# The low parts of the weights: written by ScalarE and an accumulating transfer instead of VectorE

## The chip, the cores and the metric

The kernel runs on one core of one Trainium2 chip. The metric is device time in microseconds (us), the median of several executions. The core has five engines, each with its own stream of instructions that it works off in order: TensorE (PE in the profile, its weight loads PEld), VectorE (DVE), ScalarE (ACT), GpSimd (POOL) and SyncE (SP), which here only issues transfers. Sixteen DMA engines move data between DRAM and SBUF, the on-chip memory. Matmul results land in PSUM, in eight banks.

## The reference

An encoder trunk of two layers over 512 positions of width 1024. Each layer normalises, projects once into everything that it needs, runs two kinds of attention, gates both, and projects back:

```python
for layer in range(DEPTH):                                   # DEPTH = 2
    h = rms_norm(x, norm_g[layer])
    p = h @ w_in[layer]                                      # 1024 x 6304
    c_q, c_kv, k_r, gate_a, dil_qkv, gate_b = jnp.split(p, split_points, axis=-1)
    a = mla_attention(c_q, c_kv, k_r, ..., w_uq[layer], w_ukv[layer], cos_m, sin_m) * jax.nn.silu(gate_a)
    b = dilated_attention(dil_qkv, cos_d, sin_d) * jax.nn.silu(gate_b)
    x = x + jnp.concatenate([a, b], axis=-1) @ w_out[layer]
return rms_norm(x, final_g)
```

`mla_attention` is latent attention with 8 heads: the low-rank latents are normalised and projected up by `w_uq` and `w_ukv`, with a shared rotary key. `dilated_attention` has three groups of 8 heads with strides 1, 4 and 16 and windows of 128, 512 and 2048 positions; the groups are joined by their softmax sums. Everything is float32.

## The kernel before

**Two parts for each number.** TensorE multiplies in a rounded 32-bit format (`FR`, float32r). To keep precision, activations and weights are each split into a high part, the rounded value, and a low part, the value less its high part. `triple` (lines 227 to 231) then makes a product of three matmuls into one PSUM bank: high weights by high activations (L229), high weights by low activations (L230), low weights by high activations (L231). So the low part of a weight tile is first read by the third matmul of the first triple on it.

**Weight tiles.** All weights lie in DRAM in one array `wst`, cut on the host into tiles of 128 partitions by up to 512 columns, in the order of their use: 130 tiles in each layer, 260 in all (`plan`). `prefetch` (lines 181 to 193) prepares the next tile: a transfer on SP's queue from `wst` into a raw buffer (`wraw`, three buffers, L187), ScalarE's rounding copy into the high half of a tile (`whl`, L190), and VectorE's subtraction raw less high into the low half (L191). `weight` hands tiles out, and prepares up to `AHEAD` = 3 tiles beyond the one that it hands out; `whl` has four buffers. So the casts of a tile wait until TensorE has done with the tile four places before it. The last four tiles use another buffer (`hl`). At the start two tiles are prepared after the first of the eight input blocks, and two more after the fifth.

**Work of a tile.** Most tiles hold four blocks of 128 rows by 128 columns and feed 12 matmuls of 512 columns. The first value tiles of each layer (`('v', 1, 0, i)`, eight of them) hold one block of rows by 288 columns and feed 12 matmuls of 288 columns; other value tiles feed 24 of 256.

**Order.** A planner, `Weave`, merges one main line (the projections in the order of `forward_order`, then the output projection) with side lines: norms, scores, attention outputs, joins. Fixed lags say how long after its inputs a side task may be put. The instructions then go to the engines' streams, by their place in the program and by when the builder expects them to be ready.

**What else stands on the engines near the change.** VectorE and GpSimd share the rotary step of each dilated query and key (`rope`): a shuffle (L601) and a product (L602) on VectorE, a product on GpSimd (L603), the sum on VectorE (L605 to L612), then the split into high and low (`split`, L209 on ScalarE and L210 on VectorE). In latent attention GpSimd scales the exponentials (L505), in the widest dilated group too (L740). GpSimd also adds the squares for the norms (`add_square`, L253 and L259; L341). Transposed probabilities go through `transpose_split`, which uses `split` too. The gated products (`gated`, L408) feed the output projection.

Of the kernel before, what the change touches and what calls it, by code (L numbers as in the profile page):

```python
# [8 lines left out]
FR = mybir.dt.float32r  # L9
I32 = mybir.dt.int32  # L10
AF = mybir.ActivationFunctionType
ALU = mybir.AluOpType
# [7 lines left out]
Q0, KV0, KR0, GA0, DQ0, GB0 = 0, 384, 640, 672, 1184, 5792  # L20
NG = 13
SHUF16 = [i + 16 if i < 16 else i - 16 for i in range(32)]
AHEAD, RATE, LAG, CAP = 3, 451.1, 2.5, 34.9
STEP, LD0, WARM, LG2, LY = 2, 10.0, 8, 16.5, 5.0
LV = 3.0
LG, LP, LD, LM, LC, LN, LX, LF = 6.0, 0.25, 8.25, 2.0, 14.25, 5.75, 5.0, 0.25
# [11 lines left out]
def plan():  # L38

    t = []  # L40
    for task in ORDER:
        n = {"v": 8 if task == ("v", 1, 0) else 4, "mv": 1, "muk": 1, "mur": 1, "muq": 1 - task[1] % 2 if len(task) > 1 else 0, "kr": 0}.get(task[0], 2)
        t += [("ckv", c, i) for i in range(2) for c in range(2)] if task[0] == "ckv" else [task + (i,) for i in range(n)]
    t += [("wo", n, 0) for n in range(5)] + [("wo", n, 1) for n in range(3)]
    t += [("wo", n, i) for n, i in ((5, 0), (3, 1), (4, 1), (5, 1), (6, 0), (6, 1), (7, 0), (7, 1))]
    return t
# [3 lines left out]
PLAN = plan()  # L50
# [3 lines left out]
def F(a):  # L54
    return a.bitcast(F32)
# [74 lines left out]
def hybrid_encoder(ctx, tc, xT, wst, gains, tables, keytab, masks, out):  # L130
    nc = tc.nc
# [8 lines left out]
    def t(shape, dtype, tag, bufs):  # L140
        uid[0] += 1
        return sb.tile(shape, dtype, name=f"{tag}_{uid[0]}", tag=tag, bufs=bufs)

    def hl():
        return t([128, 2, S], FR, "hl", 14)
# [36 lines left out]
    def prefetch(upto):  # L182
        while emitted[0] < min(upto, len(queue)):
            l, i = queue[emitted[0]]
            c = WCOLS.get(PLAN[i][0] if PLAN[i][:3] != ("v", 1, 0) else "vk", 512)
            raw = t([128, 512], F32, "wraw", 3)
            nc.sync.dma_start(raw[:, :c], wst[l * len(PLAN) + i, :, :c])  # L187
            w = wtile(l, PLAN[i])
            hi, lo, src = w[:, 0, :c], w[:, 1, :c], raw[:, :c]
            nc.scalar.copy(hi, src)  # L190
            nc.vector.tensor_tensor(lo, src, F(hi), op=ALU.subtract)  # L191
            ready[(l,) + PLAN[i]] = w
            emitted[0] += 1

    def wtile(l, key):

        if l + 1 == DEPTH and key[0] == "wo" and key[1] > 5:
            return hl()
        return t([128, 2, 512], FR, "whl", 4)

    used = [0]

    def weight(*key):
        used[0] += 1
        prefetch(used[0] + AHEAD)
        return ready.pop(key)
# [79 lines left out]
    for k in range(8):  # L286
        x = ogt() if k < 6 else xl()
        nc.sync.dma_start(x, xT[128 * k:128 * k + 128])
        xs.append(x)
        take_x(layers[0], k, x)  # L290
        if k in (0, 4):
            prefetch(emitted[0] + 2)
# [622 lines left out]
    for L in layers:  # L915
        l = L.l
# [39 lines left out]
        for u in range(12):  # L956
            g, p = unit(u)
            i = at["dqk", u, 1]
            att.append((i, ("d", u), [k("dqk", u, 0), k("dqk", u, 1), k("v", g, p // 2) if g else k("nv", p)],
                        far_scores if g else near_scores, far_out if g else near_out))  # L960
        for p in range(4):
            of = {unit(u): u for u in range(12)}
            i = at["dqk", of[2, p], 1]
# [148 lines left out]
```

## Time and profile before

| | |
|---|---|
| median of 3 runs | 954.73 us (954.16 to 957.48) |
| the profiled execution, own time | 954.08 us |
| its span, first to last instruction | 952.0 us |
| TensorE busy | 918.0 us (96%) |
| VectorE busy | 802.0 us (84%) |
| ScalarE busy | 529.4 us (56%) |
| GpSimd busy | 235.1 us (25%) |
| share of the 16 DMA engines' span taken by SP's transfers | 29.6% |
| read from DRAM, written | 77.09 MB, 4.36 MB |

Matmuls overlap in TensorE's pipeline, so the time from the start of one to the start of the next is shorter than one takes by itself. Instructions that only issue a transfer or wait are not counted as busy. In the groups of instructions a row gives the line of the code, the engine, the operation, what it writes and reads, how often; then busy us and mean ns of one; then the idle time of the engine just before such instructions, and what ended most of it.

### The profile page before, as it was taken

The numbers are of one execution on the slowest core, as the hardware profiler recorded it, in microseconds if no ns is written. First come the engines' busy times: TensorE is split into PE (matmuls) and PEld (weight loads), VectorE is DVE, ScalarE is ACT, GpSimd is POOL, SyncE is SP. The second block draws the span as 40 slices with busy tenths as digits, with TensorE's granted clock in tenths as the row PEclk, the third lists the DMA queues.
The fourth block names the chain that finished last, engine by engine and source line by source line (L and its number), as shares of the span: only waits on it lengthen the run. The fifth ranks groups of instructions, "written<-read, shape, count | busy, mean of one in ns | idle before, by whom it ended". The sixth has DMA issues, their size and how long they took to land.

```text
span 952.0 us, 15779 instructions
## 1 busy us (share of the span) xinstructions
PE 918.0 (96%) x5252; PEld 781.8 (82%) x5252; DVE 802.0 (84%) x1866; ACT 529.4 (56%) x1311; POOL 235.1 (25%) x257
## 2 busy tenths in 40 slices
PE   8999999999999999998999999999999999999995
PEld 5978878988789889886897888789888888888774
DVE  6767998989988987897766889989999798879775
ACT  5534665655646655653544367565656565555452
POOL 5122142213331210122211123322342112103223
PEclk9999999999999999999999999999999999999998
DMA  6422321133222222233652321212222322222342
GB/s 232 137 76 68 82 56 53 34 94 96 56 84 68 78 57 78 67 112 89 216 156 86 97 67 43 64 34 86 72 84 65 101 65 59 69 78 78 100 133 89
DMA packets 63536, 82.46 MB, mean 87 GB/s; under 512 B 14624, under 2 KB 29792, under 8 KB 63456
## 3 DMA queue, kind: packets, MB, share of 16 engines
q1 hardware_dynamic: 63456, 81.47, 29.6%
q8 instruction: 41, 0.67, 0.3%
q14 instruction: 39, 0.32, 0.1%
HBM read 77.09 MB, written 4.36 MB: 86 GB/s over the span
## 4 chain that ended last, share of the span: by engine, by line
PE 79%; DVE 12%; issue 3%; ACT 3%; DMA 1%; SPq 0%; POOL 0%; DVEq 0%; POOLq 0%; ACTq 0%
PE bank L229 22%; PE bank L230 21%; PE bank L231 21%; PE bank L424 4%; PE bank L525 3%; DVE whl L191 2%; PE bank L719 1%; DVE pt L210 1%; PE bank L760 1%; PE bank L648 1%; DVE tmp L605 1%; DVE tmp L601 1%; DVE og L766 1%; DVE og L419 1%; DVE tmp L764 1%
## 5 line engine op out<-in xcount | busy, mean ns | idle before, releaser
L229 PE MATMUL bank<-hl,whl 128*128 128x512 f32 (+1 forms) x836 | 330.6, 397 | 8.9 <-ACT hl L209 6.0
L230 PE MATMUL bank<-hl,whl 128*128 128x512 f32 (+1 forms) x836 | 326.4, 390 | 1.5 <-DVE hl L265 1.4
L231 PE MATMUL bank<-hl,whl 128*128 128x512 f32 (+1 forms) x836 | 325.3, 390 | 0.9 <-DVE whl L191 0.7
L191 DVE TENSOR_TENSOR whl<-wraw,whl 128x512 fp32r<-128x512 f32 (+2 forms) x256 | 201.3, 790 | 50.7 <-ACT whl L190 49.4
L190 ACT CAST whl<-wraw 128x512 fp32r<-128x512 f32 (+2 forms) x256 | 151.3, 597 | 157.3 <-PE bank L231 128.3
L229 PEld LDWEIGHTS bank<-hl,whl 128*128 128x128 f32 x836 | 157.4, 189 | 41.4 <-ACT hl L209 7.5
L231 PEld LDWEIGHTS bank<-hl,whl 128*128 128x128 f32 x836 | 158.4, 190 | 35.0 <-DVE whl L191 2.4
L230 PEld LDWEIGHTS bank<-hl,whl 128*128 128x128 f32 x836 | 158.9, 190 | 31.5 <-DVE hl L265 3.7
L603 POOL TENSOR_TENSOR tmp<-tmp,sd 128x512 f32<-128x512 f32 x48 | 62.2, 1296 | 238.4 <-DVE tmp L601 196.0
L505 POOL TENSOR_SCALAR p<-p,lc 128x512 f32<-128x512 f32 x64 | 52.8, 834 | 186.1 <-DVE lc L504 163.2
L210 DVE TENSOR_TENSOR pt<-bank,pt 128x512 fp32r<-128x512 f32 x128 | 83.6, 683 | 3.5 <-ACT pt L209 2.1
L229 PE MATMUL bank<-whl,hl 128*128 128x256 f32 (+1 forms) x288 | 83.2, 290 | 0.0
L230 PE MATMUL bank<-whl,hl 128*128 128x256 f32 (+1 forms) x288 | 82.2, 286 | 0.0
L231 PE MATMUL bank<-whl,hl 128*128 128x256 f32 (+1 forms) x288 | 82.1, 285 | 0.0
L209 ACT CAST pt<-bank 128x512 fp32r<-128x512 f32 x128 | 69.4, 587 | 14.2 <-PE bank L424 13.5
L424 PE MATMUL bank<-ident,p 128*128 128x128 f32 x512 | 68.7, 276 | 0.5 <-DVE st L728 0.5
L424 PEld LDWEIGHTS bank<-ident,p 128*128 128x128 f32 x512 | 59.4, 142 | 6.3 <-issue 0.9
L732 ACT ACTIVATE p<-p,st 128x128 f32<-128x128 f32 x128 | 50.0, 393 | 21.6 <-DVE st L728 21.3
L503 ACT ACTIVATE p<-bank,nm 128x512 f32<-128x512 f32 x64 | 43.4, 683 | 23.1 <-DVE nm L500 22.9
L229 PEld LDWEIGHTS bank<-whl,hl 128*128 128x128 f32 x288 | 54.7, 190 | 0.6
L230 PEld LDWEIGHTS bank<-whl,hl 128*128 128x128 f32 x288 | 54.9, 190 | 0.4
L231 PEld LDWEIGHTS bank<-whl,hl 128*128 128x128 f32 x288 | 54.8, 190 | 0.0
(181 smaller groups left out, 1471.6 us busy)
## 6 DMA issues: line engine op xcount, KB each, us to landing
wraw<-wst SPq DMA_DIRECT2D x224, 256.0 KB, 2.6
tmp<-shd SPq DMA_DIRECT2D x32, 128.0 KB, 3.2
xl<-xT SPq DMA_DIRECT2D x10, 256.0 KB, 2.6
wraw<-wst SPq DMA_DIRECT2D x16, 144.0 KB, 2.7
wraw<-wst SPq DMA_DIRECT2D x12, 192.0 KB, 2.4
x1d<-xl SPq DMA_DIRECT2D x8, 256.0 KB, 2.0
out_dram<-p SPq DMA_DIRECT2D x8, 256.0 KB, 2.1
og<-xT SPq DMA_DIRECT2D x6, 256.0 KB, 4.9
```

What stands on the lines that cost most here:

```text
L190: nc.scalar.copy(hi, src)
L191: nc.vector.tensor_tensor(lo, src, F(hi), op=ALU.subtract)
L209: nc.scalar.copy(dst_hi, src)
L210: nc.vector.tensor_tensor(dst_lo, src, F(dst_hi), op=ALU.subtract)
L229: nc.tensor.matmul(a, w[:, 0], h[:, 0], start=first, stop=False)
L230: nc.tensor.matmul(a, w[:, 0], h[:, 1], start=False, stop=False)
L231: nc.tensor.matmul(a, w[:, 1], h[:, 0], start=False, stop=last)
L424: nc.tensor.transpose(b[:, 128 * i:128 * i + 128], x, ident)
L503: nc.scalar.activation(pt, s, AF.Exp, bias=nm[:, qb, a:a + 1], scale=1.0, accum_out=l1)
L505: nc.gpsimd.tensor_scalar(pt, pt, l1, 0.0, op0=ALU.mult, op1=ALU.add)
L603: nc.gpsimd.tensor_tensor(u, u, L.sd, op=ALU.mult)
L732: nc.scalar.activation(p4[:, j, a], p4[:, j, a], AF.Exp, scale=-1.0, bias=st[:, b, a:a + 1], accum_out=st[:, b, 2 + a:3 + a])
```

## The change

Three lines change what is done and when. ScalarE, after the rounded copy (high), writes the raw tile a second time into the low half, rounded and with its sign turned. Then a transfer issued by GpSimd reads the same tile from `wst` once more and adds it to what stands in the low half: the weights less their rounded values. VectorE no longer takes part. Tiles are prepared four ahead instead of three, with five `whl` buffers instead of four. The raw buffers stay at three; such a buffer is now free after ScalarE's second pass. The last four tiles go the same way.

```diff
-AHEAD, RATE, LAG, CAP = 3, 451.1, 2.5, 34.9
+AHEAD, RATE, LAG, CAP = 4, 451.1, 2.5, 34.9
...
             w = wtile(l, PLAN[i])
             hi, lo, src = w[:, 0, :c], w[:, 1, :c], raw[:, :c]
             nc.scalar.copy(hi, src)
-            nc.vector.tensor_tensor(lo, src, F(hi), op=ALU.subtract)
+            nc.scalar.mul(lo, src, -1.0)
+            nc.gpsimd.dma_start(lo, wst[l * len(PLAN) + i, :, :c], accum_op=ALU.add)
             ready[(l,) + PLAN[i]] = w
             emitted[0] += 1
...
-        return t([128, 2, 512], FR, "whl", 4)
+        return t([128, 2, 512], FR, "whl", 5)
```

## The prediction

> **What bounds the kernel now.** I read the page's first and fourth parts, then the costliest groups, then a table of stretches, then TensorE's waits. The page:
>
> ```profile
> span 952.0 us, 15779 instructions
> PE 918.0 (96%) x5252; PEld 781.8 (82%) x5252; DVE 802.0 (84%) x1866; ACT 529.4 (56%) x1311; POOL 235.1 (25%) x257
> ...
> PE 79%; DVE 12%; issue 3%; ACT 3%; DMA 1%; SPq 0%; POOL 0%; DVEq 0%; POOLq 0%; ACTq 0%
> ...
> L191 DVE TENSOR_TENSOR whl<-wraw,whl 128x512 fp32r<-128x512 f32 (+2 forms) x256 | 201.3, 790 | 50.7 <-ACT whl L190 49.4
> L190 ACT CAST whl<-wraw 128x512 fp32r<-128x512 f32 (+2 forms) x256 | 151.3, 597 | 157.3 <-PE bank L231 128.3
> ```
>
> TensorE is busy 918 of 952 us, so nothing that other engines save can be worth more than the 34 us in which it stands (a little more, see below). VectorE is second with 802 us, and a quarter of that, 201.3 us, is the line that the change takes away. Where does TensorE stand? The table of stretches gives, behind each stretch and its length, the busy time of PE, PEld, DVE, ACT and POOL (with instruction counts), then clock, DMA share and GB/s:
>
> ```profile
> 0.00:25.00 25.00, 20.62 (x68) 13.73 (x69) 17.18 (x17) 14.59 (x26) 14.26 (x15) 0.93 0.66 221
> ...
> 95.00:165.00 70.00, 65.74 (x379) 55.93 (x378) 63.49 (x140) 43.26 (x108) 19.26 (x18) 0.98 0.26 65
> 165.00:400.00 235.00, 233.97 (x1423) 202.65 (x1422) 208.60 (x507) 140.36 (x369) 51.95 (x59) 1.00 0.25 71
> 400.00:460.00 60.00, 56.58 (x273) 45.47 (x272) 50.97 (x115) 28.77 (x71) 14.77 (x20) 0.97 0.34 102
> 460.00:555.00 95.00, 94.05 (x488) 79.86 (x487) 69.02 (x145) 43.71 (x89) 22.63 (x20) 1.00 0.43 129
> 555.00:630.00 75.00, 71.74 (x419) 60.82 (x418) 68.84 (x164) 49.09 (x129) 20.63 (x20) 0.98 0.23 61
> ...
> 860.00:930.00 70.00, 66.20 (x372) 55.95 (x371) 56.71 (x127) 36.02 (x88) 19.42 (x25) 0.98 0.35 102
> 930.00:952.00 22.00, 11.06 (x87) 10.00 (x85) 12.76 (x47) 5.50 (x14) 7.71 (x11) 0.80 0.27 95
> ```
>
> Length less PE busy is 4.4 us at the start, 10.9 us in the tail (the last norm, which the change doesn't touch), and 4.26 + 3.42 + 3.26 + 3.80 = 14.7 us in four stretches: where dilated attention starts in each layer (95, 555) and where each layer ends (400, 860). In the long stretch 165 to 400 TensorE stands 1.0 us in 235, though VectorE is 89% busy there. So the prize lies in the four stretches, and there in VectorE's queue: it is 91% busy from 95 to 165. Who ends TensorE's waits (total us, times, longest):
>
> ```profile
> PEld bank L229 <- ACT hl L209: 7.5, 5, 2.4
> PEld bank L719 <- ACT q L209: 4.7, 4, 1.3
> PEld bank L231 <- DVE whl L191: 2.4, 4, 1.2
> ```
>
> The low parts themselves hold TensorE up for only 2.4 us. The two larger waits end in ScalarE casts, but of tiles that VectorE has just written (rope's sum at L605, the gated product at L408); VectorE's queue is what made them late.
>
> **The change, part by part.**
>
> **Taken away: VectorE's 260 subtractions.** What they take in the four stretches (busy us, times):
>
> ```profile
> 95.00:165.00 70.00, 14.87 (x17) 0.98 0.26 65
> 400.00:460.00 60.00, 11.96 (x17) 0.97 0.34 102
> 460.00:555.00 95.00, 27.50 (x35) 1.00 0.43 129
> 555.00:630.00 75.00, 15.53 (x18) 0.98 0.23 61
> 860.00:930.00 70.00, 15.17 (x20) 0.98 0.35 102
> ```
>
> From 95 to 165 VectorE falls from 63.5 to 48.6 us of 70 (69%). That shortens the queue ahead of rope and the gated products. Bounds of the gain: nothing at all (what is late next is ScalarE) and some 20 us: the 14.7 us, and as a matmul's row lasts 0.39 us while the next starts 0.23 us later (rows below), each gap shows 0.16 us short; with some 30 gaps that is 5 us more. I take 10 us, two thirds of the 14.7, since the chain in these stretches still holds the same VectorE steps, only without the subtractions between them.
>
> **Added on ScalarE: a second pass over each tile**, 260 times the cast's 0.597 us, 155 us; ScalarE goes from 529 to about 684 us (72%). From 95 to 165 it goes from 43.3 to 43.3 + 17 x 0.62 = 53.8 us of 70 (77%), still under what VectorE had. The cover is ScalarE's own slack: of the 157.3 us that it stands ahead of L190, 128.3 are waits for TensorE to give back a buffer. I cost it at nothing beside the path below; if the cover is gone, see the fourth rival.
>
> **Moved: the low part's path.** Before, a tile was ready a cast (0.62) and a subtraction (0.68 or more) after its buffer was free. Now it is cast, scaled, then GpSimd issues, then the transfer lands. The instructions that stand in for the unknown terms:
>
> ```profile
> q1 hardware_dynamic: 63456, 81.47, 29.6%
> ...
> wraw<-wst SPq DMA_DIRECT2D x224, 256.0 KB, 2.6
> ...
> L187 SPq DMA_DIRECT2D wraw<-wst x260: 327/328/660, 1.7 to 921.1; - x130
> DMA to landing us min/median/max: 2.0/2.6/5.9
> L603 POOL TENSOR_TENSOR tmp<-tmp,sd 128x512 f32<-128x512 f32 x48 | 62.2, 1296 | 238.4 <-DVE tmp L601 196.0 <-DVE ls L784 29.3 <-DVE smz L217 8.9
> ```
>
> No accumulating transfer and none issued by GpSimd is in this trace. GpSimd's time for an issue lies between SP's 0.33 us and a whole pass of its own over such a tile, 1.30; I take 1.0, nearer the pass, because GpSimd does in software what it does: 260 us, which takes it from 25% to 52% busy. Issue to landing lies between a plain load's 2.6 us and twice the slowest load, 11.8; I take 4.5: the plain load, 0.7 for the longer issue, and one more reading of 256 KB. The load of the queue: 81.47 MB took 29.6% of 16 engines, so the 66 MB that are added take 24% more if a byte costs what it costs in a load, and 48% if twice that: 54 or 78% in all. Where tiles come fastest, from 460 to 555, 35 of them in 95 us are 97 GB/s; there 129 GB/s took 43%, so these add 32% (75% in all) or, at twice the cost, 65% (108%).
>
> The Trainium skill ("Collectives: The Full Stack", section "The bandwidth ceiling: the fold count and why AG ≠ RS ≠ AR") speaks against the change here: an add inside a transfer reads two sources through one read ring and runs at half a copy's rate. By it the second number of each pair holds, and the sum below would be 956 instead of 949; this trace has no such transfer.
>
> What room is there? TensorE's pace:
>
> ```profile
> 22.09 0.39 PE L229 MATMUL bank<-hl,whl 128*128 128x512 f32 x1
> 22.32 0.40 PE L230 MATMUL bank<-hl,whl 128*128 128x512 f32 x1
> ...
> 23.48 0.56 PE L229 MATMUL bank<-whl,hl 128*128 128x288 f32 x3
> ...
> 24.00 0.30 PE L231 MATMUL bank<-whl,hl 128*128 128x288 f32 x1
> 24.13 0.29 PE L230 MATMUL bank<-whl,hl 128*128 128x288 f32 x1
> ```
>
> A usual tile feeds 12 matmuls at 0.23 us, 2.7 us (the stretch 460 to 555 has 35 tiles in 95 us, also 2.7). With five buffers a tile is given its buffer four tiles before its use, where it was three: 10.9 us against a path of 0.62 + 0.62 + 4.5 = 5.7. That leaves 5 us, in which GpSimd's queue may hold the issue back: it is queued behind rope's product (L603, 1.3 us, itself waiting for VectorE's shuffle) and behind the scalings of the softmax. Over the whole span a tile comes every 952 / 260 = 3.7 us, so mostly there is more. The other way round, a GpSimd instruction behind an issue waits until the cast and the scaling are done; these follow the release at once, so I cost that at nothing. Narrow tiles (the first value tiles, 288 columns) feed 12 matmuls at 0.13 us: four tiles are 6.3 us, against 0.43 + 0.43 + 4.5 = 5.4, and only 0.9 us are left. Eight such tiles in each layer: I add 1 us for both (bounds 0 and 8, half a microsecond a tile).
>
> **The start.** The accumulating issues of the first four tiles stand on GpSimd beside its sums of squares:
>
> ```profile
> 4.55 0.62 ACT L190 CAST whl<-wraw 128x512 fp32r<-128x512 f32 x1
> ...
> 7.15 1.04 POOL L253 TENSOR_TENSOR tmp<-og 128x512 f32<-128x512 f32 x1 [2.29 <-DMA og<-xT]
> 8.27 5.02 POOL L259 TENSOR_TENSOR tmp<-tmp,tmp 128x512 f32<-128x512 f32 x3
> 13.78 6.86 POOL L259 TENSOR_TENSOR tmp<-tmp,tmp 128x512 f32<-128x512 f32 x4 [0.50 <-ACT tmp L255]
> ...
> 13.76 2.38 DVE L191 TENSOR_TENSOR whl<-wraw,whl 128x512 fp32r<-128x512 f32 x2
> ...
> 17.74 3.45 DVE L265 SCALAR_TENSOR_TENSOR hl<-xl,gn,hl 128x512 fp32r<-128x512 f32 x2
> ```
>
> The first low part was there at 6.0 us; now it lands at 4.55 + 0.62 + 0.62 + 4.5 = 10.3, 4.3 us later. Against that, VectorE's last input tile (ending at 21.2) comes 2.4 us sooner without the two subtractions at 13.76, and TensorE ran on these tiles until 23.5. GpSimd is full from 7 to 20.6 us; four issues push the end of its sums to about 24.6, and the issue of the first narrow tile, wanted at 23.5, may stand behind them. Bounds 0 (all absorbed) and 10 us (4.3 and four issues of 1.3); I take 3.
>
> **Sum**, on the profiled execution's own time (954.08 us, 2.0 around its span): 954.1 - 10 + 1 + 3 = 948.1. The median of the three runs lies 0.65 us above that execution: 949.
>
> **The rivals.**
> *No change.* The gaps in the four stretches end in ScalarE's casts, and ScalarE takes on what VectorE gives up; half the gain, 4 to 5 us, is eaten by the start and the narrow tiles: 954. For it: 1.0 us of standing in 165 to 400 at 89% VectorE. Against: VectorE's 12% of the chain.
> *Slower: the accumulating transfers come too late in the dense stretches.* In a steady run of tiles five buffers allow one tile in (path + 2.7) / 5. That passes 2.7 us when the path is over 10.9. At twice the slowest load the path is 0.62 + 0.62 + 11.8 = 13.0 and a tile takes 3.15 us: 0.43 us each for some 65 tiles (35 in 460 to 555, the like in 25 to 95) is 28 us, with the start's 3: 985. For it: twice the reading, GpSimd's issues in order behind its other work. Against: the median load needs 2.6 us.
> *The queue is full in the dense stretch.* A byte that is added costs twice what it costs in a load. From 460 to 555 the queues then have 108% to do: 95 x 0.08 = 7.6 us longer; everywhere else they fit (25 to 95 has fewer tiles): 949 + 7 = 956. For it: two readings. Against: transfers may run later into the next, emptier stretch. (This is the skill's rule above.)
> *Slower: ScalarE.* The second pass stands ahead of casts and exponentials; 69 tiles in the four stretches are 43 us of new ScalarE work there, and a fifth of it on the path, with no gain, is 8 us: 963. For it: L190's waits hold all that is queued behind them. Against: 77% busy at most.
> *More gain.* All 20 us, start absorbed: about 935.
>
> **How the numbers follow.** This kernel's measurement can tell about 0.5% (4.8 us) from no change. Chances: forecast 0.38, no change 0.17, full queue 0.10, late transfers 0.22, ScalarE 0.08, more gain 0.05. The forecast's own range is 942 to 955, so I count an eighth of its chance as no change: faster 0.38, same 0.32, slower 0.30. The range for 8 in 10 reaches from 936 (most of the gain) to 985 (late transfers at their bound); left out are the worst of the late transfers, where every tile is bound, and a little below.
>
> **What would show it.** Right: VectorE near 600 us and ScalarE near 685; TensorE's standing in the four stretches down from 14.7 to about 5; accumulating transfers landing 4 to 5 us after issue; TensorE hardly waiting for them after 30 us. Wrong: waits of TensorE at the third matmul of a triple (L231) for a transfer into whl, in the first 40 us or from 460 to 520, mean late transfers; longer waits for L209 and L503 on ScalarE mean the third rival; landings over 11 us, or GpSimd busy over 70%, would break the forecast.

## The result and the profile after

The changed kernel takes **988.71 us** (median of 4 runs, 986.68 to 989.47). The kernel before, run beside it, takes 956.11 us (954.16 to 959.04). The ratio is 1.0328, with a 95% interval of 1.0302 to 1.0355: 32.6 us slower. The forecast was 949 us.

The page of the changed kernel shows that the change did what it says. The lines are the span, the busy time of each engine, the DMA queue that GpSimd fills (packets, MB, share of sixteen engines), the shares of the chain that ended last, GpSimd's new line, and four kinds of transfer with the median us from issue to landing. Lines of the code behind L191 carry a number one higher than before.

```profile
span 987.4 us, 16166 instructions
PE 924.1 (94%) x5252; PEld 785.9 (80%) x5252; DVE 621.9 (63%) x1606; ACT 655.6 (66%) x1571; POOL 440.9 (45%) x517
...
q0 software_dynamic: 37440, 64.50, 40.8%
...
PE 73%; DMA 10%; DVE 7%; ACT 5%; issue 3%; POOL 2%; SPq 0%; POOLq 0%; DVEq 0%; ACTq 0%
...
L192 POOL DMA_DIRECT2D whl<-wst x256 | 225.9, 901 | 351.7 <-ACT whl L191 281.8
...
wraw<-wst SPq DMA_DIRECT2D x224, 256.0 KB, 3.6
whl<-wst POOLq DMA_DIRECT2D x220, 256.0 KB, 4.9
tmp<-shd SPq DMA_DIRECT2D x32, 128.0 KB, 5.9
x1d<-xl SPq DMA_DIRECT2D x8, 256.0 KB, 3.2
```

VectorE fell from 802 to 622 us, ScalarE rose from 529 to 656, and no engine but TensorE is over two thirds busy. Yet the chain that ended last, which held 1% of transfers before, now holds 10%. Two rows at the end did not stand in the prediction at all: the softmax shares of the joined groups (`tmp<-shd`) and the residual written back (`x1d<-xl`). Before, the same rows of the page were:

```profile
tmp<-shd SPq DMA_DIRECT2D x32, 128.0 KB, 3.2
x1d<-xl SPq DMA_DIRECT2D x8, 256.0 KB, 2.0
```

Nothing was done to these transfers, and they take 2.7 and 1.2 us longer. The table of stretches says where it hurts (columns as in the prediction):

```profile
0.00:25.00 25.00, 15.30 (x48) 10.92 (x49) 9.83 (x10) 16.46 (x30) 14.94 (x19) 0.80 0.92 273
25.00:95.00 70.00, 66.83 (x365) 57.01 (x364) 31.20 (x84) 41.85 (x86) 36.25 (x42) 1.00 0.92 191
95.00:165.00 70.00, 68.28 (x394) 57.90 (x393) 52.03 (x137) 55.32 (x141) 33.21 (x37) 1.00 0.59 117
165.00:400.00 235.00, 234.01 (x1426) 202.39 (x1425) 168.07 (x439) 168.60 (x422) 101.63 (x121) 1.00 0.66 138
400.00:460.00 60.00, 50.71 (x242) 41.43 (x241) 36.41 (x101) 32.49 (x84) 23.84 (x33) 0.91 0.68 145
460.00:555.00 95.00, 84.27 (x400) 69.25 (x399) 37.59 (x87) 53.52 (x110) 43.86 (x47) 0.95 0.85 196
```

From 95 to 165 TensorE stands 1.7 us instead of 4.3: here the change brings what it was forecast to. From 165 to 400 the DMA engines are 66% busy and TensorE loses nothing. From 25 to 95 they are 92% busy, and behind the first 10 of these 70 us TensorE loses nothing there either (the lags below). But from 400 to 460 it stands 9.3 us (3.4 before) and from 460 to 555 10.7 us (1.0 before), and from 0 to 25 it runs 15.3 us instead of 20.6.

How far each matmul lags shows this without the choice of stretches. Each matmul of a kernel was paired with the same matmul of the kernel before, each start counted from its own kernel's span start. The figure is the median lag in us over the 10 us of the time before that begin at the number above the column. All kernels of the experiments below are in the same table:

```
before-time     90    170    390    460    500    540    640    850    930
after          6.3    2.8    2.1   11.4   24.6   24.7   21.6   21.0   35.3
e2            -4.1   -9.0   -9.7  -13.8  -13.8  -14.0  -18.0  -18.7  -24.0
e9             3.4   -1.5   -2.3   -3.6   -3.6   -3.3   -5.3   -6.0   -8.4
e3             3.3   -1.1   -1.9    2.8    8.2    8.0    4.2    3.4    8.1
e4             9.3   10.0   23.8   36.6   48.0   49.7   51.3   63.4   78.3
e5             2.4    0.6    0.0   -2.3   -2.0   -2.0   -3.5   -4.0   -5.9
e6             1.9    0.0    1.2    9.2    9.8    9.8    7.0    6.3   18.6
e7             6.5    3.0    2.6    0.3    8.1    8.2    5.2    5.3    2.7
e8             8.3    7.1   18.9   19.3   20.4   22.6   23.9   35.2   38.0
e10            2.6    0.4    1.0   -2.3   -1.8   -1.6   -4.5   -5.3   -7.0
```

The changed kernel loses 6.3 us at the start: 6.1 of them by 20 us, and from there to 90 us the lag stays between 6.1 and 6.3, with the DMA engines 92% busy. It gains 3.5 where dilated attention begins. It loses 22.5 us at the seam between the layers (390 to 500), gains 3 in the second layer, and loses 14.3 at the end of it (850 to 930).

**What ends the waits in the places that lose.** The waits of the whole span (total us, times, longest):

```profile
DVE og L807 <- DMA tmp<-shd: 31.4, 12, 5.9
...
PEld bank L232 <- DMA whl<-wst: 23.7, 11, 6.5
...
DVE xl L824 <- DMA xl<-xT: 16.1, 4, 8.1
```

VectorE's product with the softmax shares (L806 before, now L807) stood 2.5 us for its transfer before, by its row among the groups of before:

```profile
L806 DVE TENSOR_TENSOR og<-og,tmp 128x512 f32<-128x512 f32 x16 | 11.0, 688 | 2.7 <-DMA tmp<-shd 2.5
```

It now stands 31.4 us, and everything behind it in VectorE's order stands too. TensorE itself stands for three reasons at the seam (420 to 500 us):

```profile
PE bank L232 <- DMA whl<-wst: 7.3, 2, 6.1
...
PE bank L761 <- DVE pt L211: 5.0, 1, 5.0
...
PE bank L230 <- ACT hl L210: 4.3, 1, 4.3
```

The chain of waits there (start us, us, what) shows what stands behind the three long ones:

```profile
424.00 6.11 DMA tmp<-shd
...
433.94 1.22 PE bank L230 x2
...
440.57 5.56 DMA shd<-ku
...
448.22 5.54 DMA tmp<-shd
453.85 0.69 DVE og L807
454.54 0.60 DVE tmp L409
455.17 0.70 DVE pt L211
...
470.16 5.92 DMA xl<-xT
...
476.99 5.82 DMA x1d<-xl
482.88 5.27 DMA xl<-xT
```

The shares of 424.00 release L807, a gated product (L409) and ScalarE's cast of it (L210), and TensorE's matmul at 433.94 had waited 4.3 us for that cast. The next shares go out to DRAM (`shd<-ku`) and come back spread over the partitions (`tmp<-shd`): 11.1 us of transfers, with only their issues between them. Behind their L807 in VectorE's stream stand a gated product (L409) and the low part of transposed probabilities (L211), and for that L211 TensorE waits 5.0 us at L761. Then the residual: two `xl` buffers, and a buffer is filled, added to, written out and filled again, so 5.92 + 5.82 + 5.27 us stand in a row. In the chain of before over the same work, from 400 to 476, no transfer stands at all.

The third wait, 6.1 us at L232, is for a late low part, and it is in part a consequence of this. Here are ScalarE and GpSimd at the end of this chain (start us, us, instruction, idle time before it and what ended that):

```profile
484.13 0.62 ACT L190 CAST whl<-wraw 128x512 fp32r<-128x512 f32 x1 [2.40 <-DMA wraw<-wst]
...
489.07 0.73 ACT L265 ACTIVATE hl<-xl,gn 128x512 fp32r<-128x512 f32 x1 [4.32 <-DVE xl L824]
...
491.36 0.61 ACT L191 ACTIVATE whl<-wraw 128x512 fp32r<-128x512 f32 x1
```

```profile
490.46 2.99 POOL L260 TENSOR_TENSOR tmp<-tmp,tmp 128x512 f32<-128x512 f32 x2 [7.38 <-ACT tmp L256]
493.40 2.64 POOL L192 DMA_DIRECT2D whl<-wst  x3
```

A tile was cast at 484.13. Its second pass came at 491.36, because ScalarE stood 4.32 us for the residual in between. GpSimd issued its transfer at 493.40, behind two sums of squares that had waited 7.38 us for the same residual. Its transfer landed 5.8 us later, 15.0 us after the cast. The second pass and the issue are steps in two in-order streams, and each was caught behind something else here; the landing then came on top.

### The profile page after: what moved, and what is told of

The parts are those of the page before. It is cut to its first block, busy times and chain, and to the rows that moved or that the text cites. A ratio compares the mean times of both kernels' runs of the same rounds, so it can differ in the third digit from the quotient of the medians.

```text
span 987.4 us, 16166 instructions
## 1 busy us (share of the span) xinstructions
PE 924.1 (94%) x5252; PEld 785.9 (80%) x5252; DVE 621.9 (63%) x1606; ACT 655.6 (66%) x1571; POOL 440.9 (45%) x517
## 3 DMA queue, kind: packets, MB, share of 16 engines
q0 software_dynamic: 37440, 64.50, 40.8%
## 4 chain that ended last, share of the span: by engine, by line
PE 73%; DMA 10%; DVE 7%; ACT 5%; issue 3%; POOL 2%; SPq 0%; POOLq 0%; DVEq 0%; ACTq 0%
PE bank L230 20%; PE bank L232 20%; PE bank L231 20%; PE bank L425 4%; DMA whl<-wst 3%; PE bank L526 3%; DMA tmp<-shd 2%; PE bank L761 2%; PE bank L720 1%; ACT whl L191 1%; DMA xl<-xT 1%; PE bank L649 1%; DMA shd<-ku 1%; POOL tmp L604 1%; DMA wraw<-wst 1%
## 5 line engine op out<-in xcount | busy, mean ns | idle before, releaser
L192 POOL DMA_DIRECT2D whl<-wst x256 | 225.9, 901 | 351.7 <-ACT whl L191 281.8
L232 PE MATMUL bank<-hl,whl 128*128 128x512 f32 (+1 forms) x836 | 328.9, 393 | 19.5 <-DMA whl<-wst 19.4
L232 PEld LDWEIGHTS bank<-hl,whl 128*128 128x128 f32 x836 | 159.8, 191 | 56.8 <-DMA whl<-wst 23.7
L191 ACT ACTIVATE whl<-wraw 128x512 fp32r<-128x512 f32 (+2 forms) x256 | 156.1, 610 | 0.2
L211 DVE TENSOR_TENSOR pt<-bank,pt 128x512 fp32r<-128x512 f32 x128 | 84.1, 685 | 6.7 <-ACT pt L210 5.1
L232 PE MATMUL bank<-whl,hl 128*128 128x256 f32 (+1 forms) x288 | 82.8, 287 | 0.0
L604 POOL TENSOR_TENSOR tmp<-tmp,sd 128x512 f32<-128x512 f32 x48 | 65.5, 1365 | 37.4 <-DVE tmp L602 24.3
L506 POOL TENSOR_SCALAR p<-p,lc 128x512 f32<-128x512 f32 x64 | 47.8, 753 | 66.7 <-DVE lc L505 66.5
L210 ACT CAST pt<-bank 128x512 fp32r<-128x512 f32 x128 | 70.2, 585 | 5.6 <-PE bank L425 5.2
L425 PE MATMUL bank<-ident,p 128*128 128x128 f32 x512 | 66.5, 273 | 0.0
L231 PEld LDWEIGHTS bank<-whl,hl 128*128 128x128 f32 x288 | 55.4, 192 | 5.5 <-DMA whl<-wst 5.1
L733 ACT ACTIVATE p<-p,st 128x128 f32<-128x128 f32 x128 | 49.9, 392 | 12.2 <-DVE st L729 12.1
L230 PEld LDWEIGHTS bank<-whl,hl 128*128 128x128 f32 x288 | 55.3, 192 | 0.6
```

The lines of the kernel that those rows point to most:

```text
L191: nc.scalar.mul(lo, src, -1.0)
L192: nc.gpsimd.dma_start(lo, wst[l * len(PLAN) + i, :, :c], accum_op=ALU.add)
L210: nc.scalar.copy(dst_hi, src)
L211: nc.vector.tensor_tensor(dst_lo, src, F(dst_hi), op=ALU.subtract)
L230: nc.tensor.matmul(a, w[:, 0], h[:, 0], start=first, stop=False)
L231: nc.tensor.matmul(a, w[:, 0], h[:, 1], start=False, stop=False)
```

## The experiments

In each, "before" is the kernel before on the same chip at the same time (955.65 us for e1 to e4, 956.12 for e5 to e8, 957.94 for e9 and e10). Ratios carry a 95% interval. Where two kernels are subtracted, each is first taken against its own before: +32.6 for the changed kernel, -24.6 for e2, +4.5 for e3, -12.2 for e9. By the intervals such a difference is known to some 4 or 5 us.

**e1: the longer lead alone.** The kernel before, with four tiles ahead and five buffers.

```diff
-AHEAD, RATE, LAG, CAP = 3, 451.1, 2.5, 34.9
+AHEAD, RATE, LAG, CAP = 4, 451.1, 2.5, 34.9
...
-        return t([128, 2, 512], FR, "whl", 4)
+        return t([128, 2, 512], FR, "whl", 5)
```

> The kernel before with only the look-ahead of four tiles and five whl buffers; VectorE still subtracts, no accumulating transfer. Both theories: 956 us within 4, since TensorE hardly waited for a weight tile before (2.4 us at the low parts). If more than 10 us of the loss came with the new order of instructions that the longer look-ahead brings, it would show here: 966 or more.

954.47 us against 955.65, ratio 0.9999 (0.9975 to 1.0023). The longer lead by itself is worth nothing either way that could be told (its interval is 2.3 us wide to each side). So what follows is put down to the low part's new route.

**e2: the changed kernel without the transfer.**

```diff
             nc.scalar.mul(lo, src, -1.0)
-            nc.gpsimd.dma_start(lo, wst[l * len(PLAN) + i, :, :c], accum_op=ALU.add)
```

> The changed kernel without the accumulating transfer: ScalarE writes the negated weights and that stands as the low part (left out: adding the weights, so the low parts are not the differences). It has VectorE's relief and ScalarE's second pass, and no new traffic. Theories of shared queues and of a late low part: 948 us (the two gains of about 4 us in each layer that stand in the comparison of the two traces, without the losses). Theory of ScalarE: 960 or more, and the losses at the ends of the layers (430 to 460, 910 to 935 us) stay.

931.06 us, ratio 0.9749 (0.9710 to 0.9787): faster by 24.6 us, and by 17 us more than was expected. All of ScalarE's second passes are in it, so whatever they cost is paid inside this gain, and the whole loss of the changed kernel is the transfer's: 32.6 + 24.6 = **57.2 us**. The row of the shares on its page, and its stretches at the seam:

```profile
tmp<-shd SPq DMA_DIRECT2D x32, 128.0 KB, 3.0
```

```profile
395.00:455.00 60.00, 58.94 (x285) 47.68 (x284) 40.22 (x91) 39.76 (x89) 15.29 (x22) 1.00 0.42 132
455.00:550.00 95.00, 94.21 (x492) 80.04 (x491) 48.97 (x118) 61.29 (x134) 22.82 (x20) 1.00 0.36 111
```

TensorE stands 1.1 us in the first stretch, where it stood 3.4 before; ScalarE is at 66% there. The shares land in 3.0 us, as before.

**e9: the transfer of 16 columns only.** As many issues with the same waits, but 8 KB each.

```diff
-            nc.gpsimd.dma_start(lo, wst[l * len(PLAN) + i, :, :c], accum_op=ALU.add)
+            nc.gpsimd.dma_start(lo[:, :16], wst[l * len(PLAN) + i, :, :16], accum_op=ALU.add)
```

> The changed kernel with the same 260 accumulating issues on GpSimd, at the same places and with the same waits, but each over 16 columns instead of up to 512 (left out: the addition on the other columns). GpSimd's time for issues and the fixed part of a landing stay, the bytes fall to a thirtieth. If the bytes on the shared queues cost the 58 us that the changed kernel lies above the one without transfers: 935 us, near that one's 931. If GpSimd's issues in order and the fixed latency of the low part's path are the larger part: 955 us or more.

945.70 us, ratio 0.9875 (0.9837 to 0.9914). So the issues and the fixed part of the landing cost 24.6 - 12.2 = 12.4 us (14.6 between the two medians as they are), between the two expectations. Its page:

```profile
q0 software_dynamic: 37440, 2.15, 7.0%
...
L192 POOL DMA_DIRECT2D whl<-wst x256 | 225.6, 903 | 339.0 <-ACT whl L191 263.3 <-ACT v L583 21.0 <-PE bank L232 15.6
...
whl<-wst POOLq DMA_DIRECT2D x256, 8.0 KB, 2.6
tmp<-shd SPq DMA_DIRECT2D x32, 128.0 KB, 3.1
```

Against e2 the table of lags gives 7.5 us of loss at the start (e9 less e2 at 90), 2.8 at the seam, 2.5 more by 640 and 2.9 at the end; that is 15.6 by 930, for two single executions. The shares land as before. What of it is GpSimd's order and what is the 2.6 us of an almost empty transfer isn't separated.

**e3: a plain transfer in place of the accumulating one.** Same bytes written, one reading less.

```diff
-            nc.gpsimd.dma_start(lo, wst[l * len(PLAN) + i, :, :c], accum_op=ALU.add)
+            nc.gpsimd.dma_start(lo, wst[l * len(PLAN) + i, :, :c])
```

> The changed kernel with a plain copy in place of the accumulating one (left out: the addition, so the low part is the whole weight). Same issue on GpSimd, same waits, one reading instead of two. Theory of shared queues: the new transfers' share falls from 41% towards 22%, and more than half of the loss goes: 958 to 970 us. Theory of a late low part (ScalarE's two passes and GpSimd's queue set when it is there): the landing alone gets a microsecond shorter, 978 to 988 us.

960.14 us, ratio 1.0055 (1.0030 to 1.0080). That is 4.5 + 12.2 = 16.7 us above e9, and the changed kernel is another 32.6 - 4.5 = 28.1 us above this one.

```profile
q0 software_dynamic: 37440, 64.50, 24.1%
...
whl<-wst POOLq DMA_DIRECT2D x220, 256.0 KB, 3.2
tmp<-shd SPq DMA_DIRECT2D x32, 128.0 KB, 4.3
...
L192 POOL DMA_DIRECT2D whl<-wst x256 | 142.1, 556 | 395.3 <-ACT whl L191 306.4
```

The last row shows that not only the reading differs: a plain issue holds GpSimd for 0.56 us, an accumulating one for 0.90. So the 28.1 us are the addition as a whole, its second reading and its longer issue, and the two aren't separated. Only between e9 and the changed kernel is the issue the same (0.90 both times): there the bytes, read twice, cost 12.2 + 32.6 = 44.8 us.

The shares' landing is longer the more the added transfer moves: 3.0 us without it, 3.1 narrow, 4.3 plain, 5.9 accumulating.

**e4: the transfer as pure traffic.** The kernel before, where after VectorE's subtraction a transfer adds the weights onto the raw tile. No matmul reads that tile.

```diff
-            raw = t([128, 512], F32, "wraw", 3)
+            raw = t([128, 512], F32, "wraw", 5)
...
             nc.vector.tensor_tensor(lo, src, F(hi), op=ALU.subtract)
+            nc.gpsimd.dma_start(src, wst[l * len(PLAN) + i, :, :c], accum_op=ALU.add)
```

> The kernel before (VectorE subtracts, three tiles ahead, four whl buffers) with the accumulating transfers added onto the raw buffers after their last reading, so that nothing on TensorE waits for them; five raw buffers. Only the traffic and GpSimd's issues are added. Theory of shared queues: the dependent transfers at the layer ends (shares, residual) land in 5 to 6 us as in the changed kernel: 975 to 995 us. Theory of a late low part: 955 to 962 us.

1033.13 us, ratio 1.0818 (1.0769 to 1.0868): 77.5 us slower, and worse than either theory said. Its waits:

```profile
DVE og L807 <- DMA tmp<-shd: 39.0, 12, 7.7
...
ACT whl L190 <- DMA wraw<-wst: 26.0, 13, 6.8
```

And from its page, the shares' landing:

```profile
tmp<-shd SPq DMA_DIRECT2D x32, 128.0 KB, 3.5
```

This run shows that the added transfers can cost much with no TensorE waiting for them: here no matmul reads what they write. It does not price the traffic by itself. VectorE still has its subtractions (209.3 us here), and each transfer waits for one of them in GpSimd's order. A raw buffer is held until the transfer has landed, which ScalarE feels (26.0 us for `wraw`). How the 77.5 us divide among these stays open. Part of the expectation failed: with as much added traffic as in the changed kernel (40.4% of the engines' span) the shares landed in 3.5 us, not in 5 to 6, and still VectorE stood 39.0 us for them. So that wait is not the landing's length alone; it also depends on when the shares are sent out and when VectorE comes to need them, and these weren't told apart.

**e5: VectorE keeps the first and last 24 tiles of each layer.** These are the tiles prepared around the start, the seam and the end.

```diff
-            nc.scalar.mul(lo, src, -1.0)
-            nc.gpsimd.dma_start(lo, wst[l * len(PLAN) + i, :, :c], accum_op=ALU.add)
+            if i < 24 or i >= 106:
+                nc.vector.tensor_tensor(lo, src, F(hi), op=ALU.subtract)
+            else:
+                nc.scalar.mul(lo, src, -1.0)
+                nc.gpsimd.dma_start(lo, wst[l * len(PLAN) + i, :, :c], accum_op=ALU.add)
```

> The accumulating transfers only for tiles 24 to 105 of each layer; VectorE subtracts for the first 24 and the last 24. Theory of shared queues at the layers' ends: none of the steps of loss in the changed kernel (start +6, 430 to 470 +10, 480 to 500 +13, 890 to 920 +14 us against the kernel before) is left, the two steps of gain (about 4 us each after 110 and 580 us) stay: 948 us. If the transfers cost the same wherever they are, the loss of 58 us against the kernel without them falls only in proportion, 164 of 260: about 968 us.

948.81 us against 956.12, ratio 0.9931 (0.9908 to 0.9953). Five eighths of the transfers (164 of 260) remain; the loss of 32.6 us has become a gain of 7.3. By its page the shares land in 3.8 us.

The transfers in the middle of a layer cost nothing that shows: between 170 and 390 the lag changes by 0.6 us. **Where** the transfers fall counts for far more than how many there are. At the ends the run takes away everything together: the traffic, GpSimd's issues, ScalarE's second passes and the late low parts.

**e6 and e7: one end each.** As e5, with the condition `i < 24` (e6) or `i >= 106` (e7).

> VectorE subtracts only for the first 24 tiles of each layer, the rest stays as in the changed kernel. Shared queues at the ends: the steps at the start (+6) and from 480 to 500 us (+13) go, those at 430 to 470 and 890 to 920 us stay: 970 us. Cost in proportion to the number of transfers: 978 us.

> VectorE subtracts only for the last 24 tiles of each layer (two gates' worth and the output projection). Shared queues at the ends: the steps at 430 to 470 (+10) and 890 to 920 us (+14) go, those of the start and from 480 to 500 us stay: 964 us. Cost in proportion: 978 us.

e6 gives 971.66 us, ratio 1.0181 (1.0128 to 1.0234). e7 gives 958.97, ratio 1.0030 (1.0005 to 1.0056). Against the changed kernel, taking the first 24 tiles off the transfer is worth 17.1 us, the last 24 worth 29.7. In the table e6 has no start loss to speak of (1.9) but still loses 8.0 at 390 to 460 and 12.3 at the end. e7 keeps the start loss (6.5), gains at both ends of layers, and loses 7.8 from 460 to 500, where the next layer's first tiles meet the residual's transfers. The two parts add to 46.8, more than the 39.9 that e5 is worth. The wait of e6 for the shares:

```profile
DVE og L810 <- DMA tmp<-shd: 32.1, 13, 5.8
```

In e6 VectorE waits for the shares as long as in the changed kernel (31.4); in e7 it waits 15.2 us, and they land in 3.6 us by the median. So it is mainly the transfers of a layer's last tiles that delay them.

**e8: GpSimd subtracts, with no transfer at all.**

```diff
-            nc.scalar.mul(lo, src, -1.0)
-            nc.gpsimd.dma_start(lo, wst[l * len(PLAN) + i, :, :c], accum_op=ALU.add)
+            nc.gpsimd.tensor_tensor(lo, src, F(hi), op=ALU.subtract)
```

> No transfer and no second pass: GpSimd subtracts high from raw for all tiles, some 1.3 us each. VectorE is relieved as in the changed kernel, ScalarE has its load of before, GpSimd goes from 235 to some 570 us busy. If VectorE's relief alone brings the gain seen without the transfer (931 us), and GpSimd's queue has room: 935 to 942 us. If work queued behind an instruction that waits on GpSimd is what costs (rope's product, the softmax scalings), this shows it without any new traffic: 960 us or more.

991.84 us, ratio 1.0373 (1.0330 to 1.0416). It takes the same instructions off VectorE as e2, and GpSimd is only 55% busy. Its rows of groups and of waits:

```profile
L191 POOL TENSOR_TENSOR whl<-wraw,whl 128x512 fp32r<-128x512 f32 (+2 forms) x256 | 321.1, 1264 | 291.9 <-ACT whl L190 250.7 <-issue 40.0 <-POOL q L487 0.8
```

```profile
DVE tmp L605 <- POOL tmp L603: 63.8, 30, 4.3
```

VectorE's wait for rope's product on GpSimd was 5.0 us before and is 23.6 in e2. Each subtraction stands in GpSimd's order until ScalarE's cast has come (250.7 us of idle time), with rope behind it. The transfer's issue stands in the same place for 0.9 instead of 1.26 us, so work behind a waiting issue is delayed in the same way; how much of e9's 12.4 us that makes, this run doesn't say. It also shows that VectorE's wait for the shares needs no added transfer: 16.3 us here, where they land in 3.1.

**e10: fewer tiles kept.** As e5 with `i < 12 or i >= 114`.

> As the kernel with transfers for tiles 24 to 105 only, but for tiles 12 to 113 (VectorE subtracts for the latent and first value tiles and for the output projection alone). The stretch from 25 to 95 us has no dependent transfers and wide tiles, so more relief for VectorE should cost nothing there: 946 to 950 us. If the transfers of the tiles from 106 on, which run while the softmax shares go through DRAM, are enough to delay them: 952 to 960 us.

947.19 us against 957.94, ratio 0.9894 (0.9858 to 0.9930). It is the fastest of the kernels that leave nothing out, and 4% below the changed one. Its interval overlaps e5's, so which of the two conditions is better isn't settled.

## Why the prediction was wrong, point by point

**The engines: right.** VectorE "near 600" is 622 us, ScalarE "near 685" is 656. GpSimd's issue, estimated at 1.0 us, is 0.90, and GpSimd is 45% busy, not 52%. The landing, estimated at 4.5 us, is 4.9.

**"Taken away" (-10, bounds 0 and -20): mis-sized.** With the transfer gone (e2) the lags fall by 4.9, 4.1, 4.0 and 5.3 us in the four stretches, 18.3 together. That is close to the bound, not to the value taken. The working said that the chain holds the same VectorE steps still; but in the stretch 395 to 455 of e2 TensorE stands 1.1 us in all. Another 4.1 us come at the start, which the prediction had seen as standing time but counted under no gain.

**"Added on ScalarE" (nothing): no cost shows.** e2 holds every second pass and is 24.6 us faster, more than the 20 us that the prediction set as the most that VectorE's relief could bring. The rival *ScalarE* falls with it. (Its four stretches hold 17 + 17 + 18 + 20 = 72 tiles by the prediction's own rows, not 69; that moves its price by less than half a microsecond.)

**"Moved: the low part's path" (+1): the step that failed.** Its number for the landing held, and so did the room for full tiles: even the slowest landing, 8.7 us, with two passes of 0.62 makes 9.9 of the 10.9 us that five buffers give. For the narrow tiles the room was used up: they landed in 5.5 us by the page's median, which with two passes of 0.43 makes 6.4 against 6.3. The landings of the low parts:

```profile
DMA to landing us min/median/max: 3.2/4.8/8.7
```

Two things were missing.

First, the step weighed the added load only against what the low part itself needs ("54 or 78% in all") and let the rest of the kernel's transfers stand at their old times. Between e9 and the changed kernel, whose transfers differ only in their width (2 and 64 MB), the bytes cost 44.8 us. By the lags, 23.8 us of that fall between 390 and 500 and 16.7 between 850 and 930, and of the rest 2.9 at the start, though the added transfers run everywhere. The first of these places holds the chains shown above, transfer behind transfer with an in-order engine at the end of each. The chain at the second holds the shares again: 6.32 us at 902.97, then 4.92 out and 6.37 back from 919.19 on. There a landing that is 2.7 us longer can be paid once per link, by all that is queued behind. That the bytes cost this time, and that they cost it in these two places, is measured. That they do so through VectorE's waits for the shares and the residual is read from the trace of the changed kernel; it was tested only by moving the transfers away (e5, e6, e7), which takes the late low parts and the issues away too. Giving the shares or the residual another route wasn't tried, so this last step stays likely and not shown.

Second, it took the casts, passes and issues to follow the release of a buffer "at once". The timeline at 484 to 493 shows 9.3 us between a cast and its issue, since ScalarE's and GpSimd's streams hold other work in between. e9 prices the fixed part, with the start's, at 12.4 us.

**"The start" (+3, bounds 0 and 10): in its bounds, mis-sized.** The lag is 6.3 us at 90, and against e2 10.4. The first tile's low part was put at 10.3 us; TensorE's first wait for one ended at 13.68:

```profile
6.30 1.00 POOL L192 DMA_DIRECT2D whl<-wst  x1 [4.99 <-ACT whl L191]
```

```profile
13.68 0.79 PE L232 MATMUL bank<-hl,whl 128*128 128x512 f32 x1 [5.20 <-DMA whl<-wst]
```

The issue at 6.30 came about when forecast. Its landing did not: it came after 7.3 us. The added bytes are the smaller part of this, for in e9 the first transfer, of 8 KB, was issued at 6.26 and TensorE waited almost as long:

```profile
12.10 0.80 PE L232 MATMUL bank<-hl,whl 128*128 128x512 f32 x1 [4.59 <-DMA whl<-wst]
```

So most of it was there without the added bytes: the engines were 66% busy in the first 25 us before, 76% in e9 and 92% here. The prediction took a landing in mid-kernel for one among the input blocks.

**The rivals.** *Late transfers in the dense stretches*, 985, has the side, and named the signal: TensorE at L232 waits 23.7 us for the low part, 7.4 of it in the first 40 us, 9.5 at the seam and 6.1 after 930. That its number comes so near is luck: it put 28 us on landings of 11.8 us all through two dense stretches, and the slowest was 8.7. A path over 10.9 us does occur (the 15.0 us of the tile cast at 484.13), but by the queues and at the layer's end; and the waits for the shares stand outside this rival. *Full queue*, 956, took the right cause and charged it to the wrong place: it asked whether the queue's work fits into the stretch (it does, 85% from 460 to 555 and 92% at most, from 25 to 95), not what a busy queue does to the time of each transfer. The rule behind it comes near. The Trainium skill ("Collectives: The Full Stack", section "The bandwidth ceiling: the fold count and why AG ≠ RS ≠ AR") has the adding step of a collective run at half a copy's rate, because the add needs two source reads. Here, for one core's own transfers, the same 64.50 MB took 24.1% of the engines' span plain (e3) and 40.8% accumulating: 231 against 403 us, 1.74 times and not twice.

The time's account, from the kernel before:

```
VectorE's relief, ScalarE's second pass included (e2)              -24.6
issues in GpSimd's order and the landing's fixed part (e9 - e2)    +12.4
bytes moved once, issue 0.56 instead of 0.90 us (e3 - e9)          +16.7
second reading, issue 0.90 instead of 0.56 us (after - e3)         +28.1
sum                                                                +32.6
```

## What to carry to other kernels

A transfer added to a kernel can lengthen others that are in flight with it, as it did the shares here (5.9 us for 3.2). So look not at the mean load of the DMA engines, but for chains of dependent transfers whose last link is waited for in an in-order queue that the busy engine needs, and keep added traffic away from those stretches. Here a load of 66% was free in the middle of a layer and one of 92% behind the start, and 68 to 85% cost over 20 us at one seam; leaving the change out of 28 of 130 tiles of each layer (e10) turned 3.3% slower into 1.1% faster. And a step that passes through two more in-order queues can be held in each: here a low part's transfer was issued 9.3 us after the tile's cast, though ScalarE was 66% and GpSimd 45% busy.

## What the runs showed of the hardware

- An accumulating issue over the 128 rows of a tile takes 0.90 us of GpSimd whether a row holds 512 columns or 16 (901 and 903 ns); a plain one takes 0.56 (e3). The landing of a full tile took 4.9 us accumulating and 3.2 plain, that of 8 KB accumulating 2.6.
- A DMA load of 66% over 235 us left TensorE's work untouched, and so did one of 92% from 25 to 95 us once the start was over. Yet over the whole span loads of 256 KB landed in 3.6 instead of 2.6 us and the 128 KB shares in 5.9 instead of 3.2. The smaller transfer suffered more; the runs don't say why.
- Standing costs twice here. The granted clock was 0.91 from 400 to 460 and 0.95 from 460 to 555 in the changed kernel, and 1.00 in both stretches of e2. After the 5.0 us of standing that ended at 455.92, the chain has matmuls some 0.43 us apart from 457.57 to 459.26, and 0.23 from there on. Over the span the clock was 0.973 against 0.995, and the same 5252 matmuls keep TensorE busy for 924.1 us against 908.2.
